# Activation combinations formed on GpSimd from rejoined parts, and two more plain blocks ahead of the first pair, in a hybrid attention and convolution encoder block

## The chip, the core and the metric

The kernel runs on one core of one Trainium2 chip. The core has a matrix engine (TensorE, PE in the profile, with its weight loads listed as PEld), three engines for element-wise work (VectorE as DVE, ScalarE as ACT, GpSimd as POOL), and SyncE (SP), which here issues most of the DMA transfers. Each engine works through its own queue of instructions in order, and the engines meet through semaphores. Matrix products are written to PSUM, eight banks of 128 x 512 floats; GpSimd is used in this kernel on tiles in SBUF alone. The metric is the device time of one execution in microseconds.

## The reference, cut to what matters

One encoder layer is applied to two batches of 512 tokens with the same weights. For each of them:

```python
h = rms_norm(x, norm_g)
proj = jnp.einsum('bsd,de->bse', h, w_in)
c_q, c_kv, k_rope, gate_a, conv_in, gate_c, mg_a, mg_c = split_columns(proj)
...
u = conv_in[..., :CONV_WIDTH] * jax.nn.sigmoid(conv_in[..., CONV_WIDTH:])
u = depthwise_conv(u, width 31) + dw_bias
u = jax.nn.silu(layer_norm(u, conv_ln_g, conv_ln_b)) * jax.nn.silu(gate_c)
y_c = jnp.einsum('bsc,cd->bsd', u, w_pw2)
merged = jax.nn.sigmoid(mg_a) * y_a + jax.nn.sigmoid(mg_c) * y_c
return x + jnp.einsum('bsd,de->bse', merged, w_out)
```

The part that matters is the first projection, h (1024 tokens by 1024) times the columns of w_in, in column blocks of 128, and the depthwise convolution over 31 neighbouring tokens that follows two of its parts. The attention branch y_a and the merge come later and are not touched.

## The kernel before

Every float32 matrix is used as a sum of a high and a low part of a reduced float type: the high part is a ScalarE cast, the low part the float32 value less the high part. A product is then three matrix products, high by high, high by low and low by high. The normalised activations are held transposed, as tiles `hH[k, b]` and `hL[k, b]` of 128 channels by 512 tokens, for k in 0 to 7 and batch b in 0 and 1.

**The projection.** One column block of w_in is either *plain* or half of a *pair*. A plain block (`single`, L339; `block_mm`, L317) takes 48 matrix products of 512 columns: eight k, two batches, three part-products each. A pair (`seven`, L357) multiplies two column blocks by the activations at once with seven sub-products instead of eight, in the manner of Strassen: the four quarters of the activations are b11 (k below 4, batch 0), b12 (k below 4, batch 1), b21 and b22 (k from 4, batches 0 and 1), and a pair needs them in four combinations, `TH[n, k]` and `TL[n, k]` for n = 1 to 4 and k = 0 to 3, beside the plain hH and hL. With `sums` (L137) it forms matching combinations of the two weight blocks, on GpSimd. A pair takes 84 matrix products. The order of its sub-products is: plain quarter with entry 0 of the pair, combination 2 with entry 0, combination 3 and combination 1 with entry 1, then two plain quarters with entry 2, and combination 4 with entry 3. VectorE makes four corrections in PSUM on the way (L379 v, L380, L384, L391).

**The combinations** are t1 = b12 - b11, t2 = b22 - t1, t3 = b12 - b22 and t4 = b21 - t2. Before the change, `whole_x` (L279) rejoins the batch 0 tiles on GpSimd, `xw[k]` = hH + hL, and `combine_x` (L283) takes the batch 1 values straight from the PSUM banks in which TensorE has just transposed them: ScalarE scales b22, VectorE forms t1 to t4 from PSUM and SBUF operands, ScalarE casts each to TH, and VectorE subtracts to give TL (L296). The same VectorE queue makes the low parts hL (L304) from the same banks. The transposes of batch 1 use banks of two pools: `p1` (two single banks) for even k and a two-bank tile of `pp` for odd k, always k together with k + 4.

**The order of the work.** `plan` (L194) lists six plain blocks, cb0, ca0, cb1, ca1, ma0 and ma1, then sixteen pairs, of which six make convolution inputs (cb_j, ca_j for j = 2 to 7) and ten make gates, alternating at first; then eight plain blocks (`singles`, L195). The first two plain blocks are done apart: their batch 0 half while batch 1 is still being normalised, their batch 1 half beside the transposes. From cb1 on (L505) TensorE's order is written out by hand, down to the last six plain blocks (`tail`, `NLN`, L201), which run with the layer norm that follows the convolution. The other engines are ordered by a planner that simulates a timeline with priorities: `ensure` (L162), which prepares weights some entries ahead, has a high one, and the corrections of the pairs have a smaller advance.

**Weights** stream in through three `raw` buffers on the SP queue; there are three `whi` and three `wlo` buffers, so that the split of an entry waits until TensorE is done with the one three places before it. The subtraction of a plain block's split (L129) is on VectorE for blocks 0 to 3, in `ensure` on GpSimd from block 4 on. The scratch tiles of the weight sums (s1 to s4) share their buffers, one of each, with the t tiles of the combinations.

**The convolution.** `take` (L487) forms u = ca * sigmoid(cb) on VectorE (L498) after a ScalarE sigmoid (L491). `conv_ops` (L401) does the first tap's product on ScalarE (L403) and the other thirty on VectorE (L409), 128 x 1024 each, with a running sum in PSUM; the first of them reads the ScalarE result from SBUF. There are eight channel blocks, one after another, and y of each goes to DRAM (L411). The layer norm reads y back for all channels (L535) and TensorE transposes it (L541), behind the first plain block of the tail.

## Time and profile before

| what | value |
|---|---|
| time, median of 3 runs | 1171.41 us (1171.3 to 1173.46) |
| the profiled execution | 1175.04 us, its span 1173.3 us |
| TensorE granted clock, mean | 0.987 |
| DVE busy, 42.35 to 56.81 us | 14.46 us |
| POOL busy, 80 to 100 us | 5.11 us |
| DMA traffic | 109.52 MB, mean 93 GB/s |

The span is the profiler's window of one execution on the core; the time includes what lies around it. The five busy rows of the page are averages over stages of quite different kinds: the front up to about 60 us, the pairs up to 412 us, the layer norm and pointwise product, the attention from about 700 us, and the output product. An engine's busy time counts its instructions only while they run. A time in brackets behind an instruction, as in [3.70 <-DVE u L498], is how long the engine stood idle in front of it and what released it.

### The profile page before, as it was taken

What the parts mean: (1) busy time and instruction counts of PE and PEld (TensorE: products, weight loads), DVE (VectorE), ACT (ScalarE), POOL (GpSimd) and SP (SyncE); (2) the same over time, 40 slices, a digit from 0 to 9 for tenths busy, and PEclk for the clock granted to TensorE, in tenths of its full rate; (3) what the DMA queues carried; (4) which work ended last, traced back from release to release, by engine and by line L of the source; (5) the groups of instructions that cost most, each with busy time, mean ns of one, the idle gap of its engine ahead of it and who ended that gap; (6) DMA issues with size and microseconds to landing.
All of it is one profiled execution on the core that took longest, in us unless ns stands there. A gap on an engine that the chain in (4) does not pass through costs nothing.

```text
span 1173.3 us, 15056 instructions
## 1 busy us (share of the span) xinstructions
PE 1136.8 (97%) x5796; PEld 962.9 (82%) x5796; DVE 784.7 (67%) x1156; ACT 504.2 (43%) x944; POOL 365.6 (31%) x318
## 2 busy tenths in 40 slices
PE   6799999999999998999999999999999999999998
PEld 5578888888888887878888897899999998888887
DVE  5999999999999994742221453787878788344311
ACT  6622434443534424860011434777676687122200
POOL 5043788787787633100000001222122221000000
PEclk9889999999999999999999998999999999999999
DMA  6012122322323346533432111110101011344431
GB/s 245 12 54 90 49 101 88 123 90 72 108 91 143 126 144 193 164 141 126 161 127 89 41 62 50 40 34 26 35 25 37 19 38 37 108 145 166 156 108 72
DMA packets 46520, 109.52 MB, mean 93 GB/s; under 512 B 3696, under 2 KB 20336, under 8 KB 46448
## 3 DMA queue, kind: packets, MB, share of 16 engines
q1 hardware_dynamic: 41552, 91.78, 23.6%
q10 hardware_dynamic: 4896, 16.78, 3.6%
q8 instruction: 45, 0.74, 0.2%
q14 instruction: 27, 0.22, 0.1%
HBM read 79.18 MB, written 29.36 MB: 93 GB/s over the span
## 4 chain that ended last, share of the span: by engine, by line
PE 88%; DVE 7%; ACT 2%; DMA 1%; issue 1%; POOL 1%; SPq 0%; ACTq 0%; DVEq 0%
PE blk L322 23%; PE pbi L322 9%; PE po L1062 7%; DVE py L409 4%; PE pbd L355 2%; PE pba L355 2%; PE pbb L355 2%; PE pbd L354 2%; PE pbb L354 2%; PE pba L354 2%; PE pba L353 2%; PE pbd L353 2%; PE pbb L353 2%; PE pt L829 2%; PE pkv L737 1%; PE pkv L738 1%
## 5 line engine op out<-in xcount | busy, mean ns | idle before, releaser
L409 DVE SCALAR_TENSOR_TENSOR py<-u,dwk,py 128x1024 f32<-128x1024 f32 x224 | 288.4, 1287 | 5.8
L128 ACT CAST whi<-raw 128x1024 fp32r<-128x1024 f32 (+3 forms) x49 | 50.0, 1020 | 234.4 <-PE blk L322 168.3
L179 POOL TENSOR_TENSOR olo<-s,ohi 128x512 fp32r<-128x512 f32 x64 | 82.2, 1301 | 21.8 <-ACT ohi L178 21.6
L129 DVE TENSOR_TENSOR wlo<-raw,whi 128x1024 fp32r<-128x1024 f32 (+2 forms) x38 | 47.2, 1243 | 57.2 <-ACT whi L128 57.2
L322 PE MATMUL pbi<-hH,whi 128*128 128x512 f32 x192 | 77.5, 404 | 3.7 <-DVE u L498 3.7
L322 PE MATMUL pbi<-hL,whi 128*128 128x512 f32 x192 | 76.3, 397 | 0.0
L179 POOL TENSOR_TENSOR olo<-raw,ohi 128x512 fp32r<-128x512 f32 x48 | 62.3, 1299 | 37.5 <-ACT ohi L178 27.8
L178 ACT CAST ohi<-raw 128x512 fp32r<-128x512 f32 x48 | 29.8, 621 | 98.1 <-POOL s L154 29.2
L322 PE MATMUL blk<-a,whi 128*128 128x512 f32 x256 | 68.4, 389 | 0.0
L178 ACT CAST ohi<-s 128x512 fp32r<-128x512 f32 x64 | 38.2, 620 | 59.6 <-POOL s L148 21.6
L248 POOL TENSOR_TENSOR rk<-sk,mhalf 128x4 f32<-128x4 f32 x16 | 17.2, 1073 | 148.9 <-DVE sk L747 148.9
L820 ACT ACTIVATE pr<-sc,nm,sqs 128x512 f32<-128x512 f32 x64 | 51.2, 801 | 28.5 <-DVE nm L818 28.4
L322 PE MATMUL blk<-hL,whi 128*128 128x512 f32 x144 | 59.3, 412 | 3.0 <-DVE hL L304 3.0
L322 PE MATMUL blk<-hH,whi 128*128 128x512 f32 x144 | 59.0, 416 | 2.4 <-ACT hH L303 2.0
L322 PE MATMUL pbi<-hH,wlo 128*128 128x512 f32 x192 | 60.1, 394 | 0.0
L322 PEld LDWEIGHTS blk<-a,whi 128*128 128x128 f32 x256 | 48.0, 188 | 9.9
L607 DVE TENSOR_TENSOR tmc<-blk,smc 128x1024 f32<-128x1024 f32 x8 | 9.8, 1225 | 65.8 <-PE blk L322 65.8
L322 PE MATMUL blk<-cH,whi 128*128 128x512 f32 x128 | 50.4, 394 | 2.4 <-ACT whi L128 2.4
L1065 DVE TENSOR_TENSOR o<-po,xr 128x1024 f32<-128x1024 f32 (+1 forms) x9 | 10.0, 1107 | 64.0 <-PE po L1062 64.0
L322 PE MATMUL blk<-cL,whi 128*128 128x512 f32 x128 | 50.3, 393 | 0.0
L322 PE MATMUL blk<-hH,wlo 128*128 128x512 f32 x144 | 49.2, 405 | 0.9 <-DVE wlo L129 0.9
L353 PE MATMUL pba<-hH,ohi 128*128 128x512 f32 x128 | 49.8, 389 | 0.0
(275 smaller groups left out, 3332.9 us busy)
## 6 DMA issues: line engine op xcount, KB each, us to landing
raw<-in_win_dram SPq DMA_DIRECT2D x53, 512.0 KB, 3.5
y_s<-y SPq DMA_DIRECT2D x8, 512.0 KB, 2.7
gc_s<-stgc ACTq DMA_DIRECT2D x8, 512.0 KB, 2.6
ga_s<-stga ACTq DMA_DIRECT2D x8, 512.0 KB, 2.6
mc_s<-stmc ACTq DMA_DIRECT2D x8, 512.0 KB, 2.6
yt<-y_s SPq DMA_DIRECT2D x8, 512.0 KB, 5.2
gt<-gc_s SPq DMA_DIRECT2D x8, 512.0 KB, 4.0
raw<-in_wp_dram SPq DMA_DIRECT2D x8, 512.0 KB, 5.1
```

The source lines that it names most:

```text
L128: nc.scalar.copy(hv, rv)
L129: (sub or DVE).tensor_sub(lv, rv, f(hv))
L178: nc.scalar.copy(hi[:, sl], src)
L179: nc.gpsimd.tensor_sub(lo[:, sl], src, f(hi[:, sl]))
L322: mm(ps[b] if isinstance(ps, list) else ps[:, b], (wlo if wl_ else whi)[:, k], xl(k, b) if xl_ else xh(k, b), start=(k == 0 and wl_ == 0 a ...
L353: mm(ps, hi[:, k], xh, start=first and k == 0, stop=False, skip_group_check=not first)
L354: mm(ps, hi[:, k], xl, start=False, stop=False, skip_group_check=not first)
L355: mm(ps, lo[:, k], xh, start=False, stop=k == 3, skip_group_check=not first)
L409: DVE.scalar_tensor_tensor(out, u[:, :, i : i + S], dwk[:, j, i : i + 1], src, op0=ALU.mult, op1=ALU.add)
L820: ACT(pr, ps, AF.Exp, bias=nm, scale=r["sq"][:, j : j + 1], accum_out=sm)
L829: nc.tensor.transpose(pt[:, kt], pr[:, kt * P : (kt + 1) * P], identf)
L1062: mm(ps[:, n], lhs[k][:, ts_], w[k][:, n * S : (n + 1) * S], start=first_, stop=last_)
```

## The change

GpSimd now rejoins both batches, 16 tiles instead of 8, each in a buffer of its own, and forms all four combinations from them, the TL subtractions included; ScalarE still makes the casts TH. VectorE and the PSUM banks have no part in the combinations any more. TH2 to TH4 and TL4 take over buffers of rejoined tiles that have been read for the last time. The batch 1 transposes use the two p1 banks alone, k with k + 1, and only hH and hL are made from them; all rejoining is traced behind them, and the combinations behind the batch 1 halves of the first two plain blocks. The hand-written order of the batch 0 evacuation and the batch 1 normalisation, which held for ScalarE and VectorE, now holds for GpSimd too. The plain blocks ma2 and ma3 move from behind the last pair to in front of the first one, and the low part of block 3's weights goes to GpSimd.

```diff
@@ ensure
-                    split(i, nc.gpsimd if i >= 4 else None)
+                    split(i, nc.gpsimd if i >= 3 else None)
@@ plan
-    plan = [("cb", 0), ("ca", 0), ("cb", 1), ("ca", 1), ("ma", 0), ("ma", 1)]
-    singles = [("ma", j) for j in range(2, 6)] + [("mc", j) for j in range(4, KD)]
+    plan = [("cb", 0), ("ca", 0), ("cb", 1), ("ca", 1)] + [("ma", j) for j in range(4)]
+    singles = [("ma", j) for j in range(4, 6)] + [("mc", j) for j in range(4, KD)]
@@ tiles
-    TH = {(n, k): tp.tile([P, S], F32R, name=f"tH{n}_{k}") for n in (1, 2, 3) for k in range(4)}
+    TH = {(n, k): tp.tile([P, S], F32R, name=f"tH{n}_{k}") for n in (1,) for k in range(4)}
...
-    xw = {k: tp.tile([P, S], F32, tag=f"t4_{k}", name=f"xw{k}") for k in range(KD)}
+    xw = {(k, b): tp.tile([P, S], F32, tag=f"x{k}_{b}", name=f"xw{k}_{b}") for k in range(KD) for b in range(2)}
@@ whole_x, combine_x
-        nc.gpsimd.tensor_add(xw[k], f(hH[k, 0]), f(hL[k, 0]))
+        nc.gpsimd.tensor_add(xw[k, b], f(hH[k, b]), f(hL[k, b]))
...
-        ACT(b22, banks[k + 4], AF.Identity, scale=g2)
-        DVE.scalar_tensor_tensor(t[1], banks[k], g1, xw[k], op0=ALU.mult, op1=ALU.subtract)
-        DVE.scalar_tensor_tensor(t[3], banks[k], g1, b22, op0=ALU.mult, op1=ALU.subtract)
-        DVE.tensor_sub(t[2], b22, t[1])
-        DVE.tensor_sub(t[4], xw[k + 4], t[2])
-        TH[4, k] = tp.tile([P, S], F32R, tag=f"t4_{k}", name=f"tH4_{k}")
-        TL[4, k] = tp.tile([P, S], F32R, tag=f"t4_{k + 4}", name=f"tL4_{k}")
-        for n in (1, 3, 2, 4):
+        nc.gpsimd.tensor_sub(t[2], b12, b11)
+        nc.scalar.copy(TH[1, k], t[2])
+        nc.gpsimd.tensor_sub(TL[1, k], t[2], f(TH[1, k]))
+        nc.gpsimd.tensor_sub(t[3], b12, b22)
+        nc.gpsimd.tensor_sub(t[2], b22, t[2])
+        nc.gpsimd.tensor_sub(t[4], b21, t[2])
+        at_ = {2: (k + 4, 1), 3: (k, 1), 4: (k, 0)}
+        TL[4, k] = tp.tile([P, S], F32R, tag=f"x{k + 4}_0", name=f"tL4_{k}")
+        for n in (2, 3, 4):
+            TH[n, k] = tp.tile([P, S], F32R, tag="x%d_%d" % at_[n], name=f"tH{n}_{k}")
             nc.scalar.copy(TH[n, k], t[n])
-            DVE.tensor_sub(TL[n, k], t[n], f(TH[n, k]))
+            nc.gpsimd.tensor_sub(TL[n, k], t[n], f(TH[n, k]))
@@ front
-    with tc.manual_schedule(engines={nc.scalar.engine, nc.vector.engine}):
+    with tc.manual_schedule(engines={nc.scalar.engine, nc.vector.engine, nc.gpsimd.engine}):
...
+    for k in range(0, KD, 2):
+        banks = {kk: x_bank(1, kk) for kk in (k, k + 1)}
+        trans_x(1, banks, banks)
+        evac_x(1, banks, banks)
     for k in range(KD):
-        whole_x(k)
-    held = {}
-    for k in range(5):
-        if k < 4:
-            if k % 2:
-                two = pp.tile([P, 2, S], F32, tag="pp", name=f"xT1_{k}")
-                held[k] = {k: two[:, 0], k + 4: two[:, 1]}
-            else:
-                held[k] = {kk: x_bank(1, kk) for kk in (k, k + 4)}
-            trans_x(1, held[k], held[k])
-            evac_x(1, held[k], held[k])
-        if k > 0:
-            combine_x(k - 1, held[k - 1])
+        for b in range(2):
+            whole_x(k, b)
     for i in (0, 1):
         block_mm(first[i], i, hh, hl, (1,))
         ensure(3 + i)
...
     used[0] = 2
+    for k in range(4):
+        combine_x(k)
```

More of the change, by code (lines that the diff above doesn't have):

```diff
@@ L283, in combine_x @@
-    def combine_x(k, banks):
-        g1, g2 = (vec[:, V_NG + q : V_NG + q + 1] for q in (k, k + 4))
-        b22 = xpool.tile([P, S], F32, tag="b22", name=f"b22_{k}")
-        t = {n: wp.tile([P, S], F32, tag=f"s{n}", bufs=1, name=f"t{n}_{k}") for n in (1, 2, 3, 4)}
-        ACT(b22, banks[k + 4], AF.Identity, scale=g2)
-        DVE.scalar_tensor_tensor(t[1], banks[k], g1, xw[k], op0=ALU.mult, op1=ALU.subtract)
-        DVE.scalar_tensor_tensor(t[3], banks[k], g1, b22, op0=ALU.mult, op1=ALU.subtract)
-        DVE.tensor_sub(t[2], b22, t[1])
-        DVE.tensor_sub(t[4], xw[k + 4], t[2])
-        TH[4, k] = tp.tile([P, S], F32R, tag=f"t4_{k}", name=f"tH4_{k}")
-        TL[4, k] = tp.tile([P, S], F32R, tag=f"t4_{k + 4}", name=f"tL4_{k}")
-        for n in (1, 3, 2, 4):
+    xw = {(k, b): tp.tile([P, S], F32, tag=f"x{k}_{b}", name=f"xw{k}_{b}") for k in range(KD) for b in range(2)}
@@ new lines, in whole_x, with combine_x @@
+    def whole_x(k, b):
+        nc.gpsimd.tensor_add(xw[k, b], f(hH[k, b]), f(hL[k, b]))
+    def combine_x(k):
+        b11, b12, b21, b22 = (xw[kk, b] for kk in (k, k + 4) for b in range(2))
+        t = {n: wp.tile([P, S], F32, tag=f"s{n}", bufs=1, name=f"t{n}_{k}") for n in (1, 2, 3, 4)}
+        nc.gpsimd.tensor_sub(t[2], b12, b11)
[8 more added lines that the diff above has]
+            TH[n, k] = tp.tile([P, S], F32R, tag="x%d_%d" % at_[n], name=f"tH{n}_{k}")
```

1 line of the change is left out of this document (removed).

## The prediction

> **What bounds the kernel now.** I read the page first: span, busy shares, and the forty slices.
>
> ```profile
> span 1173.3 us, 15056 instructions
> PE 1136.8 (97%) x5796; PEld 962.9 (82%) x5796; DVE 784.7 (67%) x1156; ACT 504.2 (43%) x944; POOL 365.6 (31%) x318
> PE   6799999999999998999999999999999999999998
> POOL 5043788787787633100000001222122221000000
> ```
>
> TensorE is busy 97% of the span. The change leaves its matrix products as they are and only reorders them, so time can come only from the roughly 36 us in which TensorE is idle, and from stretches at a low clock. Both lie mostly in the first two slices (29 us each). So I read next who TensorE waited for.
>
> ```profile
> PE yT L541 <- DMA yt<-y_s: 4.4, 1, 4.4
> PE pbi L322 <- DVE u L498: 3.7, 1, 3.7
> PE blk L322 <- DVE hL L304: 3.0, 4, 1.3
> ```
>
> The last two belong to the place that the change edits, the activation combinations at 30 to 61 us; the first lies at 445 us, behind the convolution. The chain of waits names the limiter of the early stretch, and the windows give its size.
>
> ```profile
> 32.52 0.75 DVE hL L304
> 33.27 0.66 DVE t L288
> 33.93 1.32 DVE hL L304 x2
> 35.25 0.60 DVE tL L296
> ```
>
> ```profile
> 30.18:42.35 12.17, 8.29 (x43) 5.61 (x42) 10.92 (x18) 7.93 (x14) 0.00 (x0) 1.00 0.01 2
> 42.35:56.81 14.46, 11.95 (x38) 8.72 (x38) 14.46 (x24) 9.23 (x15) 0.47 (x6) 0.65 0.00 1
> 60.51:107.10 46.59, 46.59 (x193) 38.34 (x194) 44.26 (x35) 8.61 (x14) 15.14 (x12) 0.94 0.14 51
> 107.10:126.20 19.10, 19.10 (x85) 15.79 (x85) 16.39 (x16) 7.12 (x14) 14.89 (x12) 1.00 0.26 83
> ```
>
> The columns are length, then TensorE, weight loads, VectorE, ScalarE and GpSimd busy, then granted clock. From 42.35 to 56.81 VectorE is busy 14.46 of 14.46 us while GpSimd does almost nothing and TensorE's clock falls to 0.65: VectorE sets the pace, because the low parts hL that TensorE needs stand in its queue among the combinations. The third row is the four plain blocks in front of the first pair (11.65 us each, 10.9 us once the clock is full: 48 products every 0.227 us), the fourth the first pair (84 products in 19.1 us, which is where 0.227 is from).
>
> Then I asked whether time won at 56 us reaches the end. VectorE's timeline answers.
>
> ```profile
> 63.47 1.28 DVE L409 SCALAR_TENSOR_TENSOR py<-u,dwk,y 128x1024 f32<-128x1024 f32 x1
> 64.79 19.91 DVE L409 SCALAR_TENSOR_TENSOR py<-u,dwk,py 128x1024 f32<-128x1024 f32 x15
> ...
> 128.36 0.68 DVE L498 TENSOR_TENSOR u<-pbd,sig 128x512 f32<-128x512 f32 x1
> ...
> 137.12 0.69 DVE L379 TENSOR_TENSOR v<-pa,pbb 128x512 f32<-128x512 f32 x1 [0.26 <-PE pbb L355]
> ...
> 139.77 0.70 DVE L384 TENSOR_TENSOR pbc<-pbc,v 128x512 f32<-128x512 f32 x1 [0.16 <-PE pbc L355]
> ...
> 145.28 0.70 DVE L391 TENSOR_TENSOR pbd<-pbd,u 128x512 f32<-128x512 f32 x1 [0.97 <-PE pbd L355]
> ...
> 153.89 1.63 DVE L409 SCALAR_TENSOR_TENSOR py<-u,dwk,y 128x1024 f32<-128x1024 f32 x1
> ...
> 412.45 27.78 DVE L409 SCALAR_TENSOR_TENSOR py<-u,dwk,py 128x1024 f32<-128x1024 f32 x21
> 440.26 1.28 DVE L409 SCALAR_TENSOR_TENSOR y<-u,dwk,py 128x1024 f32<-128x1024 f32 x1
> ```
>
> ```profile
> 448.79 1.94 PE L541 MATMUL yT<-identf,yt 128*128 128x128 f32 x8 [4.42 <-DMA yt<-y_s]
> ```
>
> The convolution's taps run on VectorE from 63.47 to 441.54, 378.07 us; the store and reload of y take 7.25 us more, and TensorE, done at 444.37, waits 4.42 us for them. So up to 445 us two chains run side by side, and VectorE's is the longer by 4.4 us. The change is worth what it moves the **start of the taps**, less what it adds to VectorE's chain; TensorE's own gain alone would end in a longer wait at yT.
>
> **The change part by part.** *Combinations off VectorE.* Per k eight VectorE instructions go (two at 0.66, six at 0.60 us by the chain's rows, 4.92 us), 19.7 us for four, with four ScalarE copies b22 that had cover. What is left to do after the second batch's transposes:
>
> ```profile
> 36.33 1.03 PE L272 MATMUL xT<-identf,xt 128*128 128x128 f32 x8
> ...
> 42.35 1.77 PE L272 MATMUL xT<-identf,xt 128*128 128x128 f32 x8 [1.48 <-DVE t L289]
> ...
> 48.87 0.63 PE L322 MATMUL blk<-hH,whi 128*128 128x512 f32 x1
> 49.30 0.63 PE L322 MATMUL blk<-hL,whi 128*128 128x512 f32 x1
> ...
> 56.42 0.39 PE L322 MATMUL blk<-hH,wlo 128*128 128x512 f32 x1
> 60.51 0.80 PE L322 MATMUL pbi<-hH,whi 128*128 128x512 f32 x1 [3.70 <-DVE u L498]
> ```
>
> ```profile
> 31.80 1.85 ACT L303 ACTIVATE hH<-xT,vec 128x512 fp32r<-128x512 f32 x3 [3.38 <-PE xT L272]
> ...
> 60.95 1.25 ACT L403 ACTIVATE y<-u,vec,dwk 128x1024 f32<-128x1024 f32 x1
> ```
>
> Only two PSUM banks now serve the transposes. One turn of the two: hH from 31.80, two pieces at 0.58, two hL at 0.66 to 0.75 behind the first, done after 2.1 us, then eight transposes at 1.03: 3.2 us. TensorE's own work in such a turn is 1.03 + 12 products of 0.227 = 3.75 us, so it becomes the limit: from 32.5, three turns of transposes (3.1) and 48 products (10.9) end at about 46.5, the last starting at 46.4 where it started at 56.42. **10.0 us earlier.** The floor is where banks alone limit (31.8 + 4 x 3.2 = 44.6, and 1.4 of products: 46.0); the ceiling is no gain at all.
>
> *From there to the first tap.* Weight cast, table load, sigmoid and u stay: 4.09 us from 56.42 to 60.51. The tap behind them was late.
>
> ```profile
> 61.10 2.45 DVE L296 TENSOR_TENSOR tL<-t,tH 128x512 fp32r<-128x512 f32 x1 [0.65 <-ACT tH L295]
> ```
>
> ```profile
> 60.62 2.38 POOL L129 TENSOR_TENSOR wlo<-raw,whi 128x1024 fp32r<-128x1024 f32 x1 [16.57 <-ACT whi L128]
> ```
>
> ScalarE had delivered the first tap's input at 62.20, but a last combination held VectorE to 63.5. It goes: 1.25 us more, in all 11.25. The weight split of block 3 that leaves VectorE (1.2 us) lay beside the sigmoid and counts nothing. The same rows show a clash: a VectorE instruction with two SBUF inputs took 2.45 instead of 0.69 us beside a GpSimd one. The Trainium skill ("GPSIMD Engine Reference", section 1, Specifications) says that GpSimd shares its SBUF interfaces with VectorE, with contention for VectorE instructions that have two SBUF inputs; these rows agree, and by it the taps whose running sum lies in PSUM would be spared. The taps of the row at 412.45 come every 1.32 us, mostly with GpSimd idle, and the fifteen at 64.79, with a split and four weight sums beside them, every 1.33. Only a first tap of each channel block reads two SBUF tensors (1.63 at 153.89 against 1.28); two of them now fall beside a full GpSimd, bounded by 0 and 2 x 1.76 us (the tL row). I take 1.0.
>
> *Two plain blocks moved to the front.* TensorE's work stays. But u2, the third block's input, comes from the first pair, now 21.8 us later behind its first tap's start. Before, u2 was complete at 129.04, 68.53 us after the singles began at 60.51. After, that is 90.3 us, plus 1.7 for ScalarE's first product, less the 1.7 between 60.51 and 62.2: channel block 2 can begin 90.3 us after the first tap. Before it began at 153.89 - 63.47 = 90.4. So it is no later, but by then VectorE had also done the second pair's four corrections (4 x 0.60 plus the waits 0.26, 0.16 and 0.97 around them, 3.8 us); these now come behind. **3.7 us given back.** Bounds: 0, if VectorE's in-order waits shrink by as much, and 5 if the first pair's waits grow too.
>
> *GpSimd's load.* Its adds and subtractions, and what it waits for:
>
> ```profile
> 15.16 10.98 POOL L281 TENSOR_TENSOR xw<-hH,hL 128x512 f32<-128x512 f32 x8 [3.33 <-DVE hL L304]
> ...
> 67.80 1.29 POOL L154 TENSOR_TENSOR s<-raw,raw 128x512 f32<-128x512 f32 x1
> 69.05 1.29 POOL L148 TENSOR_TENSOR s<-raw,s 128x512 f32<-128x512 f32 x1
> ...
> 404.56 2.40 POOL L129 TENSOR_TENSOR wlo<-raw,whi 128x1024 fp32r<-128x1024 f32 x1 [2.34 <-ACT whi L128]
> ```
>
> ```profile
> POOL olo L179 <- ACT ohi L178: 49.4, 31, 8.4
> ```
>
> At 1.25 us from start to start, 16 rejoinings (eight already there) and 32 combination steps make 60 us. The first eight have room at 15 to 26 us, the others follow hL and end near 46. Behind that stand 32 x 1.25 = 40, five weight splits at 2.40 = 12, and four instructions of the first pair's weights = 5: done at 103 plus waits. The first pair begins at 50.5 + 46.6 + 21.8 = 119, and needs combination 2 at 122. **Cover: about 16 us.** Each of the 16 steps TL waits for a ScalarE copy; at nothing each that costs nothing, at the mean of 1.6 us (49.4 / 31) 25.5 us. I take few, since a combination has other steps to do meanwhile. The splits of blocks 3 to 7 each have two plain blocks (21.8 us) before TensorE needs them. The SP queue's loads keep their order and wait for raw buffers, which the splits now free a little later; with the DMA share at 0.14 in this window that has cover. The moved blocks' two stores on ScalarE's queue go with them.
>
> **Sum:** 10.0 + 1.25 - 1.0 - 3.7 = 6.5 us. TensorE then reaches yT at 50.5 + 383.9 = 434.4 and waits about 7.9 us there. The profiled execution took 1175.04 us (span 1173.3, 1.74 around it), which is 3.6 above the median 1171.41 of the runs shown. I subtract from the median: **1164.9**; the span of a profile like this one would be 1166.8. The likeliest case's own range is 1161 to 1169, from a front 2 us quicker or 4 us slower.
>
> **The rivals.**
> *The front stays slow* (0.20): TensorE's clock falls again while it waits for banks. For it: it fell at 42.35 after a stretch 68% busy (8.29 of 12.17) whose longest gap was 1.48 us, and products then came every 0.43 us (48.87 to 49.30). Against it: the new stretch is some 90% busy. Price: 36 products at 0.2 us, 7.2: time 1172. The Trainium skill ("TensorE: Matmul & The Clock Gate", section What's actually happening) has the clock fall after an idle window of about 3.4 us; by it neither stretch should fall, and the sum would stand. The trace disagrees for the old one, so the rival keeps its chance.
> *GpSimd is late for the first pair* (0.11): the TL waits at 1.6 us eat 25.5 us against the cover of 16, so u2 and with it channel block 2 slip by 9.5; if the eight first rejoinings also stand behind others, 10 more. From 6.5 us past the cover the change loses: 1164.9 + 9.5 = 1174.4, at worst 1184. For it: GpSimd works strictly through its queue, and the splits stand in it among the combinations. Against it: it has other steps of the same combination to do while a copy is made, and its slices from 29 to 117 us are at 0, 4 and 3 tenths now. The Trainium skill ("GPSIMD Engine Reference", section 4.1, Engine selection) advises VectorE for such element-wise work, GpSimd being about twice as slow; the rows agree (1.25 to 0.60), and by that advice alone the change would lose.
> *Nothing is given back* (0.14): VectorE's waits for products in the pairs shrink with the new order, and block 2 starts without an idle stretch: 1160 or a little below.
>
> **How the numbers follow.** Forecast 0.55, the rivals 0.20, 0.11, 0.14. The measurement tells about 0.2% (2.3 us) from no change. Faster: 0.55 + 0.14 and a little of the slow front, 0.70. Same: the slow front, 0.18. Slower: late GpSimd and the rest, 0.12. Range 1159 to 1173: the late GpSimd and the extremes lie outside.
>
> **What would show it.** Right: the last plain product of the second batch at 45 to 48 us, the first tap at 51 to 54, block 2's first tap 90 us later with VectorE idle a few us before it, no TensorE wait before the first pair, and a wait at yT of 7 to 9 us near 442. Wrong: granted clock under 0.9 between 33 and 47; a TensorE wait for GpSimd or for tH near 119; or the wait at yT gone, which would mean that VectorE's chain was not the bound.

## The result and the profile after

The changed kernel takes 1167.02 us (median of 9 runs, 1163.49 to 1170.25). The kernel before, run beside it, took 1173.46 us (9 runs, 1170.57 to 1175.73). The ratio is 0.9949, with a 95% interval of 0.9931 to 0.9967: faster by 0.5%, and the interval excludes no change. The prediction said 1164.9 us and a gain of 6.5 us; the medians differ by 6.44 us, and the profiled spans, 1173.3 and 1167.2 us, by 6.1 us. The sum came out nearly exact. The terms for what is lost on the way did not, and that their errors cancel is luck.

The head of the page of the changed kernel (span, busy time by engine, slices of 29 us in tenths):

```profile
span 1167.2 us, 15046 instructions
PE 1132.9 (97%) x5796; PEld 960.7 (82%) x5796; DVE 771.3 (66%) x1123; ACT 501.6 (43%) x940; POOL 420.2 (36%) x359
...
PE   6899999999999988999999999999999999999998
...
POOL 5869687888788842100000002222222221000000
```

The move of the work shows plainly: VectorE is 13.4 us less busy, GpSimd 54.6 us more, and GpSimd's second to fourth slices, 0, 4 and 3 tenths before, are at 8, 6 and 9. TensorE gained where it was slow, in the second slice. The windows of the changed kernel (length, then TensorE, weight loads, VectorE, ScalarE and GpSimd busy, granted clock, DMA share, GB/s), for the front and for a stretch that will be needed below:

```profile
30.09:46.87 16.78, 15.66 (x81) 11.96 (x79) 7.29 (x11) 7.19 (x11) 13.52 (x12) 1.00 0.01 2
52.29:62.00 9.71, 9.71 (x35) 7.75 (x35) 9.68 (x2) 1.57 (x3) 8.97 (x7) 0.77 0.34 108
```

In the front VectorE is busy less than half of the time and the clock stays at 1.00. TensorE's timeline gives the time won:

```profile
46.48 0.39 PE L323 MATMUL blk<-hH,wlo 128*128 128x512 f32 x1
50.96 0.80 PE L323 MATMUL pbi<-hH,whi 128*128 128x512 f32 x1 [4.10 <-DVE u L494]
```

The last plain product of the second batch starts at 46.48 instead of 56.42 us, 9.94 earlier. Now VectorE's timeline, where the taps begin:

```profile
52.29 9.67 DVE L410 SCALAR_TENSOR_TENSOR py<-u,dwk,y 128x1024 f32<-128x1024 f32 x1 [1.38 <-ACT y L404]
62.00 19.91 DVE L410 SCALAR_TENSOR_TENSOR py<-u,dwk,py 128x1024 f32<-128x1024 f32 x15
81.82 1.28 DVE L494 TENSOR_TENSOR u<-pbi,sig 128x512 f32<-128x512 f32 x2
...
132.17 0.68 DVE L380 TENSOR_TENSOR v<-pa,pbb 128x512 f32<-128x512 f32 x1
...
142.44 0.68 DVE L494 TENSOR_TENSOR u<-pbd,sig 128x512 f32<-128x512 f32 x1
143.04 1.27 DVE L410 SCALAR_TENSOR_TENSOR y<-u,dwk,py 128x1024 f32<-128x1024 f32 x1
144.44 1.29 DVE L410 SCALAR_TENSOR_TENSOR py<-u,dwk,y 128x1024 f32<-128x1024 f32 x1
```

This is the surprise. The first tap starts at 52.29, 11.18 us earlier than before, and then takes **9.67 us** where 1.28 is usual, so that the second tap comes at 62.00, only 2.79 us earlier than the 64.79 of before. Yet block 2's first tap comes at 144.44 instead of 153.89, 9.45 us earlier. So of the 8.4 us that the first tap lost, 1.7 are left 92 us later. From the first tap to block 2 VectorE has no wait of more than 0.13 us: in this kernel its own queue, the held tap included, sets block 2. GpSimd's timeline beside that tap:

```profile
51.18 2.40 POOL L129 TENSOR_TENSOR wlo<-raw,whi 128x1024 fp32r<-128x1024 f32 x1
53.52 1.29 POOL L297 TENSOR_TENSOR tL<-t,tH 128x512 fp32r<-128x512 f32 x1
...
59.58 1.30 POOL L286 TENSOR_TENSOR t<-xw,xw 128x512 f32<-128x512 f32 x1
61.61 1.50 POOL L288 TENSOR_TENSOR tL<-t,tH 128x512 fp32r<-128x512 f32 x1 [0.73 <-ACT tH L287]
...
84.97 1.30 POOL L288 TENSOR_TENSOR tL<-t,tH 128x512 fp32r<-128x512 f32 x1 [6.14 <-ACT tH L287]
...
108.01 2.56 POOL L297 TENSOR_TENSOR tL<-t,tH 128x512 fp32r<-128x512 f32 x2
110.51 1.31 POOL L148 TENSOR_TENSOR s<-raw,s 128x512 f32<-128x512 f32 x1
```

GpSimd has work without a gap from before the tap's start to 60.88 and then pauses for 0.73 us; the tap, 1.28 us of work, ends at 61.96, 1.08 us after the pause began. The last row but one is the last combination, done at 110.57.

The end of the convolution, from SyncE's and TensorE's timelines: y of the last block is stored, read back, and transposed.

```profile
433.42 0.33 SPq L412 DMA_DIRECT2D y_s<-y  x1
436.39 0.38 SPq L531 DMA_DIRECT2D yt<-y_s  x1
```

```profile
441.95 1.94 PE L537 MATMUL yT<-identf,yt 128*128 128x128 f32 x8 [7.20 <-DMA yt<-y_s]
```

The store is issued 8.15 us earlier (433.42 against 441.57), the transpose starts 6.84 us earlier (441.95 against 448.79), and TensorE's wait there grew from 4.42 to 7.20 us.

### The profile page after: what moved, and what is told of

Read it like the earlier page. It is cut to its first block, busy times and chain, and to the rows that moved or that the text cites. A ratio compares the mean times of both kernels' runs of the same rounds, so it can differ in the third digit from the quotient of the medians.

```text
span 1167.2 us, 15046 instructions
## 1 busy us (share of the span) xinstructions
PE 1132.9 (97%) x5796; PEld 960.7 (82%) x5796; DVE 771.3 (66%) x1123; ACT 501.6 (43%) x940; POOL 420.2 (36%) x359
## 4 chain that ended last, share of the span: by engine, by line
PE 90%; ACT 2%; DVE 2%; DMA 1%; POOL 0%; issue 0%; ACTq 0%; DVEq 0%; SPq 0%
PE blk L323 22%; PE pbi L323 11%; PE po L1058 7%; PE pbd L356 2%; PE pba L356 2%; PE pbb L356 2%; PE pbd L354 2%; PE pba L354 2%; PE pbb L354 2%; PE pbd L355 2%; PE pba L355 2%; PE pbb L355 2%; PE pt L825 2%; PE pkv L733 1%; PE pkv L735 1%; PE pkv L734 1%
```

## The experiments

Two theories stood first. **A**: block 2 cannot begin before u2, which comes from TensorE's first pair, so what VectorE loses before that is hidden in time in which it would stand idle, and the moved blocks are there to give GpSimd time. **B**: the tap held for 9.67 us costs the end its 8.4 us. All edits below are made to the changed kernel unless another is named.

**1. The first tap without its second SBUF input.** ScalarE writes block 0's first product into PSUM, so the first tap reads it there like all the others.

```diff
-        ACT(y[j], u[:, :, 0:S], AF.Identity, scale=dwk[:, j, 0:1], bias=vec[:, V_DB + j : V_DB + j + 1])
         yt = py.tile([P, 2, S], F32, tag="py", name=f"py{j}")
+        y0 = yt if j == 0 else y[j]
+        ACT(y0, u[:, :, 0:S], AF.Identity, scale=dwk[:, j, 0:1], bias=vec[:, V_DB + j : V_DB + j + 1])
...
-            src = y[j] if i == 1 else yt
+            src = y0 if i == 1 else yt
```

> The changed kernel, with one edit: ScalarE writes the first tap's product of channel block 0 into the PSUM tile of the running sum, so that VectorE's first tap of that block reads one SBUF tensor instead of two (it took 9.67 us in the changed kernel, beside a GpSimd that ran without a gap). Theory A (what sets channel block 2 is u2, which comes from TensorE's first pair; the 8.4 us that the tap lost are hidden under that wait): the tap falls to about 1.3 us, VectorE then stands idle some 7 to 8 us in front of the first tap of block 2, that tap still begins at 144 to 145 us, and the time stays within 1 us of the changed kernel: ratio to the kernel before 0.993 to 0.997. Theory B (VectorE's chain is bound by its own work from the first tap on, so the lost 8.4 us reach the end): block 2 begins near 136 and the time falls by 6 to 8 us more, ratio 0.987 to 0.990.

Measured: 1167.49 us (1166.98 to 1169.91), ratio 0.9957 (0.9941 to 0.9972): no gain over the changed kernel. VectorE's timeline of this run:

```profile
51.92 21.23 DVE L411 SCALAR_TENSOR_TENSOR py<-u,dwk,py 128x1024 f32<-128x1024 f32 x16 [1.35 <-ACT py L406]
75.14 1.29 DVE L495 TENSOR_TENSOR u<-pbi,sig 128x512 f32<-128x512 f32 x2 [1.98 <-PE pbi L323]
...
129.77 0.69 DVE L380 TENSOR_TENSOR v<-pa,pbb 128x512 f32<-128x512 f32 x1 [4.17 <-PE pbb L356]
...
140.05 0.68 DVE L495 TENSOR_TENSOR u<-pbd,sig 128x512 f32<-128x512 f32 x1
140.65 1.27 DVE L411 SCALAR_TENSOR_TENSOR y<-u,dwk,py 128x1024 f32<-128x1024 f32 x1
142.34 1.29 DVE L411 SCALAR_TENSOR_TENSOR py<-u,dwk,y 128x1024 f32<-128x1024 f32 x1 [0.42 <-ACT y L406]
```

All sixteen taps of the first row take 1.3 us each beside the same full GpSimd: it was the form with **two SBUF inputs** that was held. The time saved turns into waits for TensorE (1.98 and 4.17 us) and for ScalarE's product of block 2 (0.42), none of which stand in the rows of the changed kernel at the same places, and block 2 starts only 2.10 us earlier. It starts 90.42 us behind the first tap, where 90.3 had been worked out for u2, and 92.15 in the changed kernel. The transpose at the end comes at 441.55 against 441.95. A holds, though it wanted block 2 at 144 to 145; B falls.

Differences of one or two us between two profiles need care, since each is one execution: pbi, the first product of TensorE's hand-written order, starts at 50.96 in the changed kernel's profile and anywhere from 49.52 to 50.76 in those of its variants. The edit also does more than it says. The tile of the running sum has one buffer and is now asked for ahead of ScalarE's product, and the product of block 1 moves behind a number of casts in ScalarE's queue: it starts at 93.09 instead of 83.14 us. That matters for number 8.

**2 to 4. The moved blocks.** Number 2 moves one plain block, number 3 none, and number 4 makes that part of the change alone, two blocks moved in the kernel before.

```diff
# 2
-    plan = [("cb", 0), ("ca", 0), ("cb", 1), ("ca", 1)] + [("ma", j) for j in range(4)]
-    singles = [("ma", j) for j in range(4, 6)] + [("mc", j) for j in range(4, KD)]
+    plan = [("cb", 0), ("ca", 0), ("cb", 1), ("ca", 1)] + [("ma", j) for j in range(3)]
+    singles = [("ma", j) for j in range(3, 6)] + [("mc", j) for j in range(4, KD)]
# 3: range(2) and range(2, 6)
# 4, in the kernel before: range(4) and range(4, 6)
```

> The changed kernel with one plain block moved ahead of the first pair instead of two (the other stays behind the last pair). The first pair begins 10.9 us sooner, near 108, if GpSimd's combinations are ready by then (in the changed kernel the last of them ended at 110.5). Theory A: u2 comes near 132, but VectorE, whose first tap still loses 8.4 us, ends block 1 only near 145 to 147, so the start of block 2 hardly moves and the time is within 1.5 us of the changed kernel, ratio 0.993 to 0.997; TensorE waits 0 to 4 us for combinations at the first pair, which costs nothing. Theory B (the front's gain decides alone, the place of the plain blocks does not matter): the same time, but with no wait at the first pair and block 2 at 144.

> The changed kernel with the plan of before: no plain block is moved, so that the first pair would begin near 97.4 while GpSimd is still forming combinations (in the changed kernel it formed the last of them at about 110). Theory A: TensorE waits 8 to 14 us at the first pair, mostly for combination 2, arrives as much later behind the last pair, near 445 instead of 434.7, and the wait at yT is gone; the time is 2 to 5 us above the changed kernel, ratio 0.996 to 1.000. Rival C (GpSimd's load has cover enough without the two blocks, since it would do its combinations first): no wait at the first pair, ratio 0.992 to 0.996.

> The kernel before with the other part alone: two more plain blocks in front of the first pair, combinations still on VectorE from PSUM. Theory A: the front is as before (first plain block of the hand-written order at 60.5, first tap at 63.5), u2 comes at 60.5 + 92.2 = 152.7, block 2 begins at 154 as before, and the corrections of the second pair fall behind it: 0 to 4 us slower than the kernel before, ratio 1.000 to 1.004, with VectorE idle 4 to 6 us in front of block 2. Rival D (the place of the two blocks is what brings the gain): ratio 0.994 to 0.997.

Number 2: 1166.38 us (1164.08 to 1168.88), ratio 0.995 (0.9934 to 0.9966), no different from two blocks. Its first tap took 9.68 us, TensorE waited 1.2 us at the first pair, and block 2 came at 145.84, about where A had it.

Number 3: 1173.94 us, scattered from 1167.85 to 1185.99, ratio 1.0009 (0.9985 to 1.0033): the gain is gone. The wait that A expected at the first pair, 8 to 14 us, came to 24.0 in the profiled run: a miss in size. That run took 1182.57 us, 8.6 above the median of the twelve, so its waits need not be those of a middling one. Its timelines of VectorE, ScalarE, GpSimd and TensorE, one row each:

```profile
50.92 23.27 DVE L410 SCALAR_TENSOR_TENSOR py<-u,dwk,y 128x1024 f32<-128x1024 f32 x1 [1.38 <-ACT y L404]
```

```profile
95.37 1.24 ACT L404 ACTIVATE y<-u,vec,dwk 128x1024 f32<-128x1024 f32 x1 [21.91 <-DVE u L494]
```

```profile
97.20 1.28 POOL L288 TENSOR_TENSOR tL<-t,tH 128x512 fp32r<-128x512 f32 x1 [21.86 <-ACT tH L287]
```

```profile
121.88 0.80 PE L354 MATMUL pbb<-tH,ohi 128*128 128x512 f32 x1 [24.01 <-ACT ohi L178]
```

Read downwards, this is a chain through four engines. The tap was held 23.27 us, and u of block 1 stands behind block 0's taps in VectorE's queue. ScalarE's first product of block 1 waited for that u, and the casts tH stood behind it in ScalarE's queue; GpSimd waited for a cast, and TensorE for what follows it. This is read from one trace; the link at ScalarE is that block 1's product stands in front of the casts. In the changed kernel the same chain runs, shorter: ScalarE's row there is

```profile
83.14 1.25 ACT L404 ACTIVATE y<-u,vec,dwk 128x1024 f32<-128x1024 f32 x1 [6.79 <-DVE u L494]
```

and the 6.14 us of GpSimd's row at 84.97 above are its other end. There the moved blocks covered it.

Number 4: 1177.04 us (1173.99 to 1178.96), ratio 1.0033 (1.0019 to 1.0046). Moving the blocks alone costs 4 us, at the upper end of what A allowed; the theory that they bring the gain falls. The way is not the one that A named, for in the profile block 2 came at 149.97 instead of 154, and where the 4 us are lost isn't known.

**5, 6 and 8. Both findings joined.** Number 5 is 1 and 2 together; number 8 is 1 and 3 together, so nothing is moved and the first tap reads PSUM. Number 6 has the first tap in PSUM and makes block 2's input from plain blocks: cb2 and ca2 stand behind cb1 and ca1, and ma2 and ma3 become a pair in their place.

```diff
# 6
-    plan = [("cb", 0), ("ca", 0), ("cb", 1), ("ca", 1)] + [("ma", j) for j in range(4)]
+    plan = [("cb", 0), ("ca", 0), ("cb", 1), ("ca", 1), ("cb", 2), ("ca", 2), ("ma", 0), ("ma", 1)]
...
-    for j in range(2, KD):
+    twos.append((("ma", 2), ("ma", 3)))
+    for j in range(3, KD):
```

> The changed kernel with both edits: one plain block moved instead of two, and the first tap's product of channel block 0 in PSUM. Theory A (the start of channel block 2 is the later of two: u2 from the first pair, and the end of block 1 on VectorE; each edit alone moves only one of them, so each alone gave nothing): block 2 begins at 137 to 141 instead of 144.4, y of the last block is stored near 429 to 431 instead of 433.4, the wait at yT falls to 1 to 4 us, and the time is 3 to 5 us below the changed kernel: ratio to the kernel before 0.990 to 0.993. Theory A' (VectorE's in-order waits for the pairs' products grow by what is won): ratio 0.994 to 0.997 again.

> The changed kernel with the PSUM tap of block 0, and with the four moved or kept plain blocks chosen otherwise: behind ca1 come cb2, ca2, ma0 and ma1 as plain blocks, and ma2 with ma3 becomes a pair in place of cb2 with ca2. TensorE's count of products is the same; u2 is ready near 95, long before VectorE needs it. Theory A: VectorE has no idle stretch in front of block 2, which begins near 131 to 133; the remaining corrections then all lie behind it, y is stored at 427 to 431, and the ratio is 0.989 to 0.993. Theory A': 0.994 to 0.997.

> The version with no plain block moved (0.9985 to 1.0033, first tap 23.3 us, TensorE 24.0 us idle at the first pair) with the first tap's product of block 0 in PSUM. Theory S (the held tap is what stopped ScalarE, which waited for u1 from VectorE, then GpSimd, which waited for ScalarE's casts, then TensorE): the tap takes 1.3 us, ScalarE's and GpSimd's 22 us waits go, TensorE waits 4 to 10 us at the first pair, ratio 0.991 to 0.997. Rival G (GpSimd has too much to do in front of the first pair without the two blocks, tap or no tap): TensorE still waits 15 us or more, ratio 0.998 to 1.003.

| | median us (range) | ratio (95%) | block 2's first tap | yT starts, wait there |
|---|---|---|---|---|
| changed kernel | 1167.02 (1163.49 to 1170.25) | 0.9949 (0.9931 to 0.9967) | 144.44 | 441.95, 7.20 |
| 5: one block, tap in PSUM | 1162.32 (1160.0 to 1165.31) | 0.9916 (0.9896 to 0.9936) | 143.51 | 439.44, 5.12 |
| 6: cb2, ca2 plain, tap in PSUM | 1163.14 (1161.66 to 1164.73) | 0.9925 (0.9908 to 0.9942) | 141.79 | 438.12, 5.00 |
| 8: no block, tap in PSUM | 1163.0 (1160.99 to 1165.4) | 0.9923 (0.9906 to 0.9941) | 144.23 | 441.69, 0.36 |

All three medians are some 4 us below the changed kernel's, which ran in another set; the intervals of the ratios still touch (0.9931 against 0.9936 to 0.9942), and the three aren't told apart from one another. All three beat both kernels by their medians. In 5 and 6 block 2 did not come at 137 to 141 and at 131 to 133, as I had expected: with u2 earlier, VectorE's own queue became the limit. In 6 it ran from 50.89 to 141.79 with 60 taps of some 1.33 us (79.6 us), the rest being u, corrections, and waits in order for TensorE's products (5.7 us in five places). So A explains why 1 and 2 brought nothing, but not the gain of these three, of which the start of block 2 has only 0.93, 2.65 and 0.21 us. Their profiled spans are 4.6, 5.9 and 7.1 us shorter than the changed kernel's. Of that, 2.51, 3.83 and 0.26 are there at the start of yT, and the rest arises behind it.

Number 8 against number 3 is the sharpest pair of the study. The edit between them is the one of number 1, and the ratios, 0.9923 and 1.0009, have intervals that don't touch: it is worth some 10 us. What TensorE waited for at the first pair of number 8, in total, times and longest, and two rows of its ScalarE:

```profile
PE pbb L354 <- ACT ohi L178: 3.1, 1, 3.1
PE pbb L356 <- POOL olo L179: 1.1, 1, 1.1
```

```profile
74.91 0.62 ACT L287 CAST tH<-t 128x512 fp32r<-128x512 f32 x1
...
93.64 1.24 ACT L406 ACTIVATE y<-u,vec,dwk 128x1024 f32<-128x1024 f32 x1
```

TensorE waits 3.1 and 1.1 us instead of 24.0. So G of its expectation falls, and GpSimd has time enough without the moved blocks. S had named the held tap as the only cause, and that is not shown: the edit cuts the chain of number 3 in two places. The tap is no longer held, and block 1's product, in front of the casts at 95.37 there, stands behind them at 93.64 here. A kernel with the hold and the product behind the casts was not run. Number 10 below has the reverse, a tap that got in and the product in front of the casts, at 74.41 us, but with the two blocks moved; TensorE did not wait for anything at its first pair.

Number 8 also shows what a wait at yT costs beside itself. It reaches the transpose at the same time as the changed kernel, but without a wait. The windows behind it, of the changed kernel and then of number 8:

```profile
440.00:450.00 10.00, 8.05 (x32) 6.86 (x33) 3.00 (x5) 0.00 (x0) 1.12 (x2) 0.71 0.96 247
```

```profile
440.00:450.00 10.00, 9.64 (x55) 8.08 (x55) 3.87 (x7) 3.74 (x6) 4.65 (x5) 1.00 0.93 261
```

After the wait of 7.20 us the granted clock is 0.71, after one of 0.36 us it is 1.00. From the start of yT to the first gated output of the pointwise product (tmc on VectorE's timelines, at 529.08 and 525.40 us) it takes 87.13 us and 83.71 us: 3.4 us more. The other profiles agree. It is 83.74 us in number 3 behind a wait of 0.25, and 86.39 to 87.42 us in the kernel before and numbers 1, 2, 4, 5, 6, 10 and 12, behind waits of 4.42 to 7.30. On these figures the price of such a wait is some 3 us behind it, and it doesn't grow with the wait in that range. No run changes the wait alone, so the figure is a reading, not a test. Number 8 gains another 3.4 us behind tmc, which no run explains. The Trainium skill ("TensorE: Matmul & The Clock Gate", section What's actually happening) has the clock fall after an idle window of some 3.4 us; these two waits agree with it.

**7, 9 and 11. The clash by itself.** Three small kernels run a tap beside GpSimd subtractions that follow one another without a gap. The core of number 9, shortened, in which `tap` has two SBUF inputs when `src` is w2 and one when it is acc, a PSUM tile:

```python
def gps(first, n):
    for i in range(n):
        G.tensor_sub(gt[i], first if i == 0 else a, b)

def tap(out, ptr, src):
    V.scalar_tensor_tensor(out, w1, ptr, src, op0=ALU.mult, op1=ALU.add)

gps(d[2][:, :S], 12)
tap(acc, gt[0][:, 0:1], w2)
```

In number 7 each subtraction reads the result of the one before. Number 11 varies the width of the subtractions, the type of their outputs and the DMA traffic.

> Not the kernel: it only loads x, stores it unchanged, and runs short groups on VectorE and GpSimd to measure the clash; everything else of the computation is left out. Five groups: VectorE alone (three 128x512 subtractions and 128x1024 taps with two SBUF inputs or with a PSUM sum); twelve GpSimd subtractions of 128x512 without a gap beside taps whose sum is in PSUM; the same twelve beside one tap with two SBUF inputs; twelve with a ScalarE copy between the sixth and the seventh, beside a two-input subtraction and then a two-input tap; last, eight two-input taps without a gap with a GpSimd subtraction behind the fifth. Theory L (a VectorE instruction with two SBUF inputs cannot start before GpSimd pauses): in group 3 the tap takes as long as the remaining GpSimd instructions, 11 to 15 us, then 1.3; in group 4 the subtraction ends in the pause, near the sixth instruction, 6 to 8 us; the PSUM taps of group 2 keep 1.29. Theory T (the two take turns): 2.5 to 4 us in both groups.

> Not the kernel: x is loaded and stored unchanged and short groups run on VectorE and GpSimd; everything else of the computation is left out. In the earlier measurement each GpSimd subtraction read the one before it (1.33 us from start to start), and a two-input tap waited only for the one that was running (2.39 us). Here the twelve subtractions of a group do not depend on each other, as in the kernel, where they came every 1.25 us. Group 1: beside taps with a PSUM sum. Group 2: beside one tap with two SBUF inputs. Group 3: the same with a ScalarE copy in front of the seventh subtraction. Group 4: subtractions of 128x256. Group 5: the chain of the earlier run as a control. Theory L2 (GpSimd instructions without a wait between them leave no opening for a VectorE instruction with two SBUF inputs): the tap takes 13 to 16 us in group 2, 7 to 9 in group 3, 7 to 9 in group 4, and 2.4 in group 5; the PSUM taps keep 1.29. Theory T2 (it waits for the one running instruction whatever follows): 2.4 us in groups 2, 3 and 5, about 1.8 in group 4.

> This kernel leaves the block's computation out. It measures the disputed hold by itself: five groups, each a run of independent GpSimd subtractions of two SBUF inputs without a gap, and in each a VectorE 128x512 tap of two SBUF inputs that becomes ready when the first subtraction has ended, and a second tap behind it. A: the tap becomes ready while a 128x1024 subtraction runs, nine 128x512 ones behind it. B: while a 128x512 one runs, a 128x1024 one behind that. C: while the first of five 128x1024 ones runs. D is A with fp32r outputs on GpSimd, E is A with loads landing beside it. Theory W (the instruction is held when it becomes ready beside a wide GpSimd subtraction, and stays held until GpSimd makes a pause): the first tap of A takes 13 us or more, that of B 2.3 us, that of C 10 us or more, and D and E are like A. Theory T (it is held for the one GpSimd instruction that runs when it becomes ready): A 3.0 to 3.7 us, B 2.3 us, C 3.0 to 3.7 us, D and E like A. Theory R (the fp32r outputs or the loads make the hold): A and C 3.0 to 3.7 us, and D or E 13 us or more.

VectorE's timeline of number 7, a tap from PSUM and one from SBUF, each ready as GpSimd's second instruction starts:

```profile
16.66 1.29 DVE L80 SCALAR_TENSOR_TENSOR acc<-xt,g,acc 128x1024 f32<-128x1024 f32 x1 [1.38 <-POOL g L69]
...
34.06 2.39 DVE L85 SCALAR_TENSOR_TENSOR acc<-xt,g,xt 128x1024 f32<-128x1024 f32 x1 [1.38 <-POOL g L69]
```

VectorE's timeline of number 11: groups B (beside a 128x512 subtraction) and C (beside a 128x1024 one):

```profile
32.11 2.27 DVE L74 SCALAR_TENSOR_TENSOR acc<-xt,G,xt 128x1024 f32<-128x1024 f32 x1 [1.38 <-POOL G L71]
...
47.81 3.35 DVE L74 SCALAR_TENSOR_TENSOR acc<-xt,G,xt 128x1024 f32<-128x1024 f32 x1 [1.37 <-POOL G L71]
```

Groups A, D and E took 3.35 too, and in number 9 the two-input taps took 1.74 to 2.39. In all of them the tap waited for **the one GpSimd instruction that ran**, about 1 us or 2 by its width, and then went in although more work was queued (theories T and T2, with number 7's 2.39 and 2.29 just under T's 2.5 to 4). GpSimd pays in its turn: in number 9 the 128x512 subtraction behind the first held tap took 2.25 us instead of 1.26. No small kernel showed a hold over several instructions; the theories that wanted 10 us or more there (L, L2, W, R) are wrong for it.

**10 and 12. The held tap in the kernel.** Number 10 gives block 3's split back to VectorE. Number 12 makes GpSimd's 128x1024 splits as two of 128x512.

```diff
# 10
-                    split(i, nc.gpsimd if i >= 3 else None)
+                    split(i, nc.gpsimd if i >= 4 else None)
# 12
-        (sub or DVE).tensor_sub(lv, rv, f(hv))
+        if sub is nc.gpsimd and i != J["kr"]:
+            for c in range(0, n, S):
+                sub.tensor_sub(lv[:, c : c + S], rv[:, c : c + S], f(hv[:, c : c + S]))
+        else:
+            (sub or DVE).tensor_sub(lv, rv, f(hv))
```

> The changed kernel with one part undone: the low part of block 3's weights is subtracted on VectorE again, 128x1024 with two SBUF inputs, in front of u of block 0 in VectorE's queue. The prediction counted this part at nothing, as hidden beside the sigmoid. Theory L2: ready at 47.3, it either slips in before GpSimd's instruction at 47.5 (then 1.2 to 2.5 us, u0 not delayed, ratio as the changed kernel, 0.993 to 0.997) or is held as the first tap was, to a pause of GpSimd near 59, and u0, and TensorE's first block behind it, come 8 to 10 us later: ratio 1.000 to 1.006. Theory N (no holding by GpSimd; the tap's 9.67 us had another cause): 1.2 to 2.5 us and 0.993 to 0.997, with GpSimd running on without a pause while it does.

> The changed kernel, with GpSimd's splits of weights, one 128x1024 subtraction of 2.4 us each, made as two 128x512 ones. The first tap of block 0 becomes ready at about 52.3 us, beside one of these subtractions, and GpSimd has work without a gap until about 61. Theory W (the tap is held because it becomes ready beside a wide subtraction of this kernel): it gets in at the next end of a GpSimd instruction and takes 2.0 to 3.0 us, and block 0 ends some 7 us earlier than in the changed kernel, at about 93. Theory G (it is held by GpSimd's work without a gap, and how wide the instruction is does not matter): it takes 8 us or more again. By both, block 2's first tap comes within 3 us of 144.4 and the profiled span is 1161 to 1169 us, since the second half of block 2's u sets that tap.

Number 10: 1167.85 us (1164.45 to 1169.71), ratio 0.9959 (0.9942 to 0.9976), the same time as the changed kernel. But its first tap got in. VectorE's row, then GpSimd's two:

```profile
50.85 2.15 DVE L410 SCALAR_TENSOR_TENSOR py<-u,dwk,y 128x1024 f32<-128x1024 f32 x1 [1.38 <-ACT y L404]
```

```profile
50.63 1.28 POOL L297 TENSOR_TENSOR tL<-t,tH 128x512 fp32r<-128x512 f32 x1
51.87 3.39 POOL L129 TENSOR_TENSOR wlo<-raw,whi 128x1024 fp32r<-128x1024 f32 x1
```

It waited for the tL, and the next GpSimd instruction took 3.39 us instead of 2.40. This execution, 1164.45 us, is the fastest of the twelve, and the others have no trace, so the median doesn't tell what the hold costs. Block 2 came at 140.28, 89.43 us behind the first tap, with VectorE waiting 3.48 us for the pair on the way: that fits A. The split that the run gave back started at 45.86, before GpSimd's instruction at 46.01, and took 1.23 us, so it tells nothing about L2 against N.

Number 12, one run: 1167.03 us, span 1165.3 us. Its first tap, beside 128x512 subtractions only:

```profile
51.92 9.94 DVE L414 SCALAR_TENSOR_TENSOR py<-u,dwk,y 128x1024 f32<-128x1024 f32 x1 [1.38 <-ACT y L408]
```

It was held until GpSimd's next pause again, so the width isn't the cause, and W falls in the kernel too; of this run's two theories G stands. **Why the tap is held over many GpSimd instructions in four of these kernels and for one in number 10 and in the small kernels stays open.** Each is one traced execution, and whether the same kernel does either from one execution to the next isn't known. Shown is that only the two-input form is held, and that it got in, in all four, when GpSimd paused. In the changed kernel and numbers 2, 3 and 12 the pause began at 60.88, 60.67, 73.11 and 60.77 us, and the tap ended 1.08 or 1.09 us after that. In number 3 a pause of 0.42 us was enough:

```profile
73.53 1.81 POOL L179 TENSOR_TENSOR olo<-raw,ohi 128x512 fp32r<-128x512 f32 x1 [0.42 <-ACT ohi L178]
```

The moment at which the tap becomes ready doesn't decide it alone. Number 12's came 1.13 us into a 128x512 subtraction and was held 9.94 us; the first tap of block 7 in number 5 came 1.15 us into one, with another behind it, and took 1.28. The two-input first taps of blocks 1 to 7 took 2.47 us at most in all these kernels.

## Why the prediction came out as it did

*The bound.* Right. What was won at the start of VectorE's chain came through to the end, less the losses below; TensorE only waits longer at yT, and its wait there was 7.20 us at 441.95 as foreseen (7 to 9 near 442).

*The front, 10.0 us.* Right to 0.06 (9.94), which is partly chance, since pbi's start differs by up to 1.44 us among the profiles; the clock was at 1.00 where the rival of the slow front wanted less than 0.9. The first tap starts 11.18 us earlier, predicted 11.25, so the last combination in front of it was rightly priced at 1.25.

*"I take 1.0", the two first taps beside a full GpSimd.* The mechanism, a two-input tap that waits beside a full GpSimd, was right; the size was not: 8.39 us (9.67 less 1.28) for the first and 0.12 for the second, against bounds of 0 and 3.52. The bound came from rows in which VectorE had waited for one GpSimd instruction; no row of the kernel before showed one held over several, not even beside its eight GpSimd additions without a gap from 15.16 us, where two weight splits of VectorE took 1.94 and 2.19 instead of 1.23. It did not cost 8.4 us because u2 would have kept block 2 back anyway: the first experiment gives back 2.10 us of it there and nothing that can be measured at the end.

*u2 and "VectorE idle a few us before" block 2.* Not so in the changed kernel, although the number is close (92.15 us behind the first tap where 90 were predicted). The held tap had filled the idle stretch, and VectorE's own queue came 1.7 us later than u2 would have. Without the hold the predicted mechanism is there: in the first experiment block 2 comes at 90.42, and VectorE waits at u, v and y on the way, 6.6 us together. What stands behind the taps in the queues was not in the working: u of block 1, and the casts behind ScalarE's product of it, were late by the hold too, and that reached GpSimd (6.14 us) but not TensorE.

*"3.7 us given back".* Too much. From block 2's first tap to the store of the last y it takes 288.98 us after (433.42 less 144.44) and 287.68 before (441.57 less 153.89): 1.3 us. The corrections that came behind are paid, but VectorE's waits in front of corrections shrank, as the rival that nothing is given back had it. Groups of VectorE's instructions by line, of the kernel before and of the changed one (busy time, mean ns, then idle time before them and what ended it):

```profile
L409 DVE SCALAR_TENSOR_TENSOR py<-u,dwk,y 128x1024 f32<-128x1024 f32 x8 | 12.5, 1558 | 0.3
...
L391 DVE TENSOR_TENSOR pbd<-pbd,u 128x512 f32<-128x512 f32 x16 | 11.2, 698 | 7.6 <-PE pbd L355 7.5
```

```profile
L410 DVE SCALAR_TENSOR_TENSOR py<-u,dwk,y 128x1024 f32<-128x1024 f32 x8 | 23.0, 2871 | 1.9 <-ACT y L404 1.4
...
L392 DVE TENSOR_TENSOR pbd<-pbd,u 128x512 f32<-128x512 f32 x16 | 11.2, 698 | 3.5 <-PE pbd L356 3.2
```

The wait in front of pbd fell from 7.5 to 3.2 us. Another 1.3 us went where I had looked at nothing: from the store of y to yT it takes 8.53 us (433.42 to 441.95) instead of 7.22 (441.57 to 448.79). A store of a gate was issued on ScalarE's queue at 436.44, beside the reload's issue at 436.39; in the kernel before 1.5 us lay between the two. In numbers 1, 4, 10 and 12 the two issues also lie within 0.25 us and it takes 8.46 to 8.63 us; in 2, 5 and 6 they lie 1.1 to 1.2 us apart and it takes 7.38 to 7.64. That the one slows the other was not tried.

*The sum by what was measured*: 11.18 at the first tap, 9.45 at block 2, 8.15 at the store, 6.84 at yT, 6.1 at the end, where 6.5 was predicted. Losses of 5.1 us stand against 4.7 in the working, in other places.

*GpSimd's cover, "about 16 us".* The last combination was done at 110.57 instead of 103, so 8.5 us were left before the first pair at 119.07, and TensorE did not wait there: right in the outcome. The TL waits were few but for one of 6.14 us. Number 3 shows what the rival of the late GpSimd would have been: without the two blocks the same hold grows to 23.27 us in its traced execution, and the gain is gone. With number 1's edit, number 8 does without the moved blocks.

*The split of block 3 that "counts nothing".* Right: number 10, which takes it back, isn't told apart from the changed kernel.

The measured median lies 2.1 us above the forecast, and most of that is the reference: beside these runs the kernel before took 1173.46 us, not the 1171.41 from which I subtracted.

## What to carry to other kernels

Before work is put on an engine until it has no gaps, look through VectorE's queue for the few instructions with two SBUF inputs, here the first tap of each block, and move one of their inputs to PSUM: between numbers 3 and 8 the edit that did so for one tap, and with it changed the order of ScalarE's queue, was worth some 10 us. A stall on an engine that isn't the bound is free only as long as nothing that another engine's queue needs stands behind it, so follow it through the queues (VectorE, ScalarE, GpSimd, TensorE here) before calling it hidden. Look at the order in which the planner then puts the other queues before calling such an edit a change of one operand. And when time is won ahead of a join, ask what sets the next block's start: here two chains, VectorE's taps and TensorE's u2, meet within 2 us, and speeding up one alone (numbers 1 and 2) brought nothing.

## What the runs showed of the hardware

A VectorE instruction with two SBUF inputs, 1.28 us alone, took 2.15 to 2.4 us when it waited for one 128x512 GpSimd subtraction and 3.35 for one of 128x1024; held in a row of them without a gap it took 9.67, 9.68, 9.94 and 23.27 us. The GpSimd instruction behind it pays as well, 3.39 instead of 2.40 us. The same instruction with its running sum in PSUM took 1.29 us beside the same work. The Trainium skill ("GPSIMD Engine Reference", section 1, Specifications) names this contention and its condition, and the runs agree with both; how long it lasts that section does not say, and these rows do. The other unexpected figure is the clock: behind waits of TensorE of 4.42 to 7.30 us the stretch from yT to tmc took 86.4 to 87.4 us, behind waits of 0.25 and 0.36 us 83.7.
